# One weight split moved behind the layer norm, and two rounding copies moved from the vector to the scalar engine

## The chip, the cores and the metric

The kernel runs on one core of one Trainium2 chip. The metric is device time in microseconds (us) of one execution; lower is better. The engines of the core are TensorE (PE, with its weight loads listed as PEld), VectorE (DVE), ScalarE (ACT), GpSimd (POOL) and SyncE (SP, which issues most DMAs). Each engine runs its own instructions in the order in which the program gives them.

## The reference

One encoder layer for 1024 prompt frames, 64 sample frames and 16 meta tokens, all float32. A normed input goes through one projection into q, k, v, an attention gate, a GLU pair and a convolution gate. Group A is windowed attention. Group B is what this change touches; its reference is

```
def _conv_branch(u, left, conv_w, ln_g, ln_b, w_pw):
    h = _dwconv(jnp.concatenate([left, u], axis=1), conv_w)
    h = jax.nn.silu(_layernorm(h, ln_g, ln_b))
    return h @ w_pw
```

Both groups are then normed, multiplied by their gates, joined and multiplied by `w_out`; a last norm and the residual follow.

## The kernel before, in words

Float32 products are made of rounded parts. A weight or an activation is split into `hi` (the value rounded to the matmul's reduced float32 format, by a plain copy into a tile of that type) and `lo` (value minus `hi`, by a subtraction on DVE). A product is then three matmuls: hi with hi, hi with lo, lo with hi. So every operand of a matmul costs a copy and a subtraction before it may be used.

Four stages follow each other on PE. First the input projection: matmuls named `g`, in units of 24 (8 blocks of k, three parts) for each of 22 column blocks and 3 token ranges. From about 187 us on the attention (`s`, `pa`, `pb`, `av`) is woven between these units by a loop over `i`, 19 turns, in which `fill(n)` emits the next n projection matmuls. The same loop carries the layer norm of the convolution result `H` (128 partitions, 4 channel blocks, 1118 columns) in three token ranges: `ln_pre` (sums), `ln_mean`, `ln_var` (variance; DVE adds epsilon into `rln`, POOL raises it to the power -0.5), `ln_diag` (DVE writes the results on a diagonal, `sqc<-ident,rln`), and `ln_scale` (PE broadcasts them, `rstd<-sqc,ones_m`, and DVE multiplies, `H<-H,rstd`). The last range's `ln_var` comes at the end of the turn before last, its `ln_diag` and `ln_scale` in the last turn, i = 18.

The pointwise weights `w_pw` come in two blocks of 512 KB. The first, places 22 in `WORDER` (`whi`, `wlo`), is split as the projection ends. The second, place 23 (`w1kT` its hi, `w1vT` its lo), is split on DVE by `hi_w` and `lo_w` in turn 18, ahead of `ln_diag` and `ln_scale` of the last range.

After the loop `do` runs tasks by letters: `w` loads a block of `w_out`, `h` or `H` writes its hi part (on ACT or DVE), `l` its lo part on DVE and issues a later load, `S` is SiLU with the norm's gain and bias on `H` for one of four token ranges of 280 columns (ACT, 4 instructions), `z` is `split_z`, which splits that range into `zh` and `zl`, `g` is SiLU of a gate, `G` applies attention gates, `M` and `n` split the joined operand of the output product.

Then come the 16 pointwise products, n over four token ranges and m over four output blocks, 12 matmuls each (4 hi with `zh`, 4 lo with `zh`, 4 hi with `zl`). Behind each, DVE multiplies the result by the gate into `H` (`H<-pw,gb`, called H(n,m) here) and ACT squares it (`sqc<-pw` for m = 0, `csq<-pw` else, called square(n,m)). After each product the next item of a hand-written plan is emitted; a comma joins tasks of one item:

```
    plan = "G0,l1,h2 l2,h3 l3,S2 h4 z2 l4,h5 l5,S3 h6 z3,h7 l6,M0 l7 n0 r0 . M1 n1".split()
    for n in range(4):
        for m in range(4):
            pointwise(n, m, [pre[PW], pre[PW + 1]])
            do(plan[4 * n + m])
```

So `z2` follows product (1,0), and `z3` follows product (2,0). All of this is pinned to program order on each engine. Last comes the output product (`y` matmuls) for 9 token tiles, with its norm, residual and stores. All engine instructions pass through a helper, so DVE, ACT and POOL show line L86, matmuls L104, transposes L108.

Of the kernel before, what the change touches and what calls it, by code (L numbers as in the profile page):

```python
# [11 lines left out]
F32R = mybir.dt.float32r  # L12
AF = mybir.ActivationFunctionType
ALU = mybir.AluOpType

P = 128
# [6 lines left out]
KT = D // P  # L23
# [20 lines left out]
WORDER = [AT, BT, AT + 1, BT + 1, KM, AT + 2, BT + 2, VM, AT + 3, BT + 3] + [  # L44
    QT, QT + 1, QT + 2, QT + 3, GBT, GBT + 1, GBT + 2, GAT, GAT + 1, GBT + 3, GAT + 2, GAT + 3, PW, PW + 1]
# [3 lines left out]
def layer_kernel(ctx: ExitStack, tc: tile.TileContext, x, x_fm, w_in, w_pw, w_out, vec, g_post,  # L49
# [43 lines left out]
    act, dve, pool = Engine(nc.scalar, "act", 200, 0.82), Engine(nc.vector, "dve", 60, 1.18), Engine(nc.gpsimd)  # L93

    def freer():

        return "act" if given["act"] < (given["pe"] + LATE if taps else given["dve"]) else "dve"
# [16 lines left out]
    sm = ctx.enter_context(tc.tile_pool(name="sm", bufs=2))  # L114
# [21 lines left out]
    def slot(tag, name, shape=(P, 1152), dt=F32):  # L136
        return m4.tile(list(shape), dt, tag=tag, bufs=4 if tag == "B" else 2, name=name)
# [35 lines left out]
    def load_raw(p, parts=((0, KT),)):  # L173
        if p < len(WORDER) and (p not in raws or parts[0][0]):
            m = WORDER[p]
            src = w_in[m] if m < PW else w_pw[m - PW]
            if not parts[0][0]:
                raws[p] = wp.tile([P, KT, P], F32, tag="wraw", bufs=2, name=f"wraw{m}") if p != 2 else None
            for a, b in parts:
                if p == 2:  # L180
                    dst = halves[a] = sm.tile([P, 4, P], F32, tag="asq", bufs=2, name=f"wraw{m}_{a}")
                else:
                    dst = raws[p][:, a:b]
                nc.sync.dma_start(dst, src[:, a * P:b * P].rearrange("p (k c) -> p k c", c=P))
# [5 lines left out]
    def hi_w(p, on_dve=False, dst=None, a=0, b=KT):  # L190
        m = WORDER[p]
        load_raw(p)
        if not a:
            pre[m] = dst or (wp.tile([P, KT, P], F32R, tag="whi", name=f"whi{m}"),
                             wp.tile([P, KT, P], F32R, tag="wlo", name=f"wlo{m}"))
        raw, hi = halves[a] if p == 2 else raws[p][:, a:b], pre[m][0][:, a:b]
        if on_dve:
            dve.tensor_copy(hi, raw)
        else:
            act.activation(hi, raw, AF.Copy)  # L200

    def lo_w(p, a=0, b=KT, on_dve=False):
        hi, lo = (t[:, a:b] for t in pre[WORDER[p]])
        raw = halves[a] if p == 2 else raws[p][:, a:b]
        if p > 3 and not on_dve and freer() == "act":
            act.activation(lo, hi.bitcast(F32), AF.Copy, scale=-1.0)
            pool.dma_start(out=lo, in_=raw, accum_op=ALU.add)
            return
        dve.tensor_tensor(out=lo, in0=raw, in1=hi.bitcast(F32), op=ALU.subtract)
# [182 lines left out]
    def tick():  # L392
        steps[0] += 1
        run_due(lambda p: p[0] <= steps[0])
        while taps and given["dve"] < given["pe"] + AHEAD:
            f, j = taps.pop(0)
            f(j)

    def fill(k):
        for _ in range(min(k, len(queue))):  # L400
            queue.pop(0)()
            tick()
# [159 lines left out]
    def split_z(n):  # L562
        a, b = LNC[n]
        w = b - a
        hc = H[:, :, a:b]
        zh = slot("T", f"zh{n}", (P, 4, 280), F32R)
        zl = slot("P", f"zl{n}", (P, 4, 280), F32R)
        dve.tensor_copy(zh[:, :, :w], hc)
        dve.tensor_tensor(out=zl[:, :, :w], in0=hc, in1=zh[:, :, :w].bitcast(F32), op=ALU.subtract)
        zs[n] = zh, zl  # L570

# [119 lines left out]
    def att_v(c):  # L691

        if c % 2 == 0:
            nc.sync.dma_start(vE[MB:MB + HD], vtok[:HD, c // 2])
            avs[c] = [(NKEY, vE)]
            if c:
                avs[c].insert(0, (2 * HD, vcache if c == NCHUNK else vtok[:, c // 2 - 1]))
        else:
            if c > 1:
                nc.sync.dma_start(vO[:HD], vtok[HD:, c // 2 - 1])  # L700
            avs[c] = [(HD + MB, vO if c > 1 else vE), (NKEY, vtok[:, c // 2])]
# [17 lines left out]
    def att_values(c):  # L719
        sample = c == NCHUNK  # L720
        av = ps_tile("av", 1, f"av{c}")
        last = len(att[c]) - 1
        for n, (k, v, pt) in enumerate(att[c]):
            for g in range(2):
                mm(av[g * HD:(g + 1) * HD, :256], lhsT=v[:k, g * HD:(g + 1) * HD],
                   rhs=pt[:k, g * 256:(g + 1) * 256], start=n == 0, stop=n == last)
        av4 = av[:, :256].rearrange("p (t q) -> p t q", t=4)
        act.activation(qb[:, c], av4, AF.Copy)
        Tt = c // 2
        if Tt not in asq:  # L730
            asq[Tt] = sm.tile([P, 4, P], F32, tag="asq", bufs=2, name=f"asq{Tt}")
        o = (c % 2) * HD
        act.activation(asq[Tt][:, :, o:o + HD], qb[:, c], AF.Square)
        if c % 2 or sample:
            w = HD if sample else P
            s = asq[Tt]
            pool.tensor_tensor(out=s[:, 0:2, :w], in0=s[:, 0:2, :w], in1=s[:, 2:4, :w], op=ALU.add)
            pool.tensor_tensor(out=s[:, 0, :w], in0=s[:, 0, :w], in1=s[:, 1, :w], op=ALU.add)

    def att_stats(Tt):  # L740
        w = HD if Tt == 8 else P
        row_rstd(asq[Tt][:, 0, :w], w, ra[:, Tt:Tt + 1], f"ra{Tt}", mm_ps(f"ra{Tt}"))
# [139 lines left out]
    def gate_att(ready, most=12):  # L882
        for g in [g for g in gas if all(c in ready for c in range(g[2] // HD, g[3] // HD))][:most]:
            gas.remove(g)
            t, n, c0, c1, gt = g
            dst = qb[:, c0 // HD:c1 // HD, t, :]
            dve.tensor_tensor(out=dst, in0=dst, in1=chunks(gt[:, :c1 - c0]), op=ALU.mult)
# [64 lines left out]
    order = [NCHUNK] + list(range(NCHUNK))  # L952
# [5 lines left out]
    i = -1  # L958
    while (i := i + 1) < max(len(order) + 2, L0 + 7 if L0 < 99 else 0):
        left = len(order) + 1 - i  # L960
        if L0 == 99 and i >= 9 and (i == 12 or len(taps) < 2):
            L0 = i
        quota = (max(24, -(-(len(queue) - REST) // left)) if i else 48) if left > 0 else 26
        n = i - L0
        if i < len(order):
            exps, norm = att_scores(order[i])
        if n > 0:
            gate_att(order[:max(0, i - 2)], 2)
        if 3 <= i < len(order) + 3:
            c = order[i - 3]  # L970
            if c % 2 or c == NCHUNK:
                att_stats(c // 2)
        if 2 < i <= len(order) + 1:
            att_values(order[i - 2])
        if 1 < i < len(order):
            att_v(order[i])
        if i == len(order) + 1:
            hi_w(len(WORDER) - 1, on_dve=True, dst=[sm.tile([P, KT, P], F32R, tag=t, bufs=1, name=f"w1{t}")
                                          for t in ("kT", "vT")])
            lo_w(len(WORDER) - 1, on_dve=True)  # L980
        if i + 1 < len(order):
            att_prep(order[i + 1])
        fill((32 if i == 1 else 4) if left > 0 else 0)
        if 0 < i <= len(order):
            att_transpose(order[i - 1])
        if i < len(order):
            exps()
        fill(8 if left > 0 else 4)
        if n == 0:
            while taps:  # L990
                f, j = taps.pop(0)
                f(j)
            sqc = sm.tile([P, HW], F32, tag="sq", bufs=1, name="sqc")
        for step, at in ((ln_pre, (0,1,3)), (ln_diag, (2, 4, 6))):
            if n in at:
                step(at.index(n))
        if i < len(order):
            norm()
        fill(8 if left > 0 else 4)
        if i == 1:  # L1000
            att_values(order[0])
            att_v(order[1])
        for step, d in ((ln_mean, 0), (ln_var, 1), (ln_scale, 2)):
            if n - d in (0, 2, 4):
                fill(2)
                step((n - d) // 2)
        fill((quota - 20 if left > 0 else 8) - (2 if 0 <= n <= 6 else 0))

    def gb_silu(i):
        act.activation(gbs[i][:, :HW], gbs[i][:, :HW], AF.Silu)  # L1010
# [70 lines left out]
    def rc_rstd(T):  # L1081
        if T in rcs:
# [9 lines left out]
                 w=wo_load, G=lambda _: gate_att(order), H=lambda i: wo_hi(i, True))  # L1092
# [37 lines left out]
    for T in (0, 1, 8, 2, 3, 4, 5, 6, 7):  # L1130
# [40 lines left out]
        dst = y_p[t0:t0 + r] if T < 8 else y_s  # L1171
# [78 lines left out]
```

## Time and profile before

| what | value |
|---|---|
| median of 3 runs | 470.9 us (470.34 to 470.97) |
| the profiled execution: its own time | 470.69 us |
| its span, first to last instruction | 468.9 us |
| PE busy | 456.2 us (97%) |
| DVE busy | 380.1 us (81%) |
| ACT busy | 231.3 us (49%) |
| POOL busy | 75.0 us (16%) |
| mean granted TensorE clock | 0.997 |

The profiled execution takes 1.79 us more than its span and lies 0.21 us under the median. Busy shares are averages over stages with different limits, so the stage between 325 and 365 us has to be read by itself. In the listings below an instruction's start and duration are given, then its engine, the program's name of what is written and read, and in brackets the idle time of the engine before it with what ended it.

### The profile page before, as it was taken

The numbers are of one execution on the slowest core, as the hardware profiler recorded it, in microseconds if no ns is written. First come the engines' busy times: TensorE is split into PE (matmuls) and PEld (weight loads), VectorE is DVE, ScalarE is ACT, GpSimd is POOL, SyncE is SP. The second block draws the span as 40 slices with busy tenths as digits, with TensorE's granted clock in tenths as the row PEclk, the third lists the DMA queues.
The fourth block names the chain that finished last, engine by engine and source line by source line (L and its number), as shares of the span: only waits on it lengthen the run. The fifth ranks groups of instructions, "written<-read, shape, count | busy, mean of one in ns | idle before, by whom it ended". The sixth has DMA issues, their size and how long they took to land.

```text
span 468.9 us, 7427 instructions
## 1 busy us (share of the span) xinstructions
PE 456.2 (97%) x2809; PEld 416.7 (89%) x2809; DVE 380.1 (81%) x672; ACT 231.3 (49%) x534; POOL 75.0 (16%) x106
## 2 busy tenths in 40 slices
PE   7999999999999999999999999999999999999994
PEld 6999999999999999998988988797899787888884
DVE  3669999999999999999899987996999547554443
ACT  6585532135032223666766856774977335333322
POOL 0000100013000000010111113254024411111100
PEclk9999999999999999999999999999999999999998
DMA  8992144035023333330101010111252212222231
GB/s 271 402 344 117 36 105 126 0 86 153 13 68 93 89 91 91 89 94 5 48 7 49 6 52 4 48 55 42 97 175 90 91 67 91 67 92 90 97 124 48
DMA packets 16491, 43.54 MB, mean 93 GB/s; under 512 B 2600, under 2 KB 4888, under 8 KB 16456
## 3 DMA queue, kind: packets, MB, share of 16 engines
q1 hardware_dynamic: 14584, 37.31, 23.4%
q0 software_dynamic: 1872, 5.77, 6.6%
q8 instruction: 22, 0.36, 0.3%
q14 instruction: 13, 0.11, 0.1%
HBM read 32.00 MB, written 4.84 MB: 79 GB/s over the span
## 4 chain that ended last, share of the span: by engine, by line
PE 85%; DVE 8%; DMA 2%; ACT 2%; issue 1%; POOL 1%; SPq 0%; DVEq 0%; POOLq 0%; ACTq 0%
PE g L104 53%; PE y L104 20%; PE av L104 3%; PE s L104 3%; DVE wo L86 2%; DVE H L86 2%; PE pa L108 2%; PE pb L108 1%; DMA x<-in_x_fm_dram 1%; DMA woraw<-in_w_out_dram 1%; DVE wlo L86 1%; POOL sqc L86 1%; DVE qb L86 1%; DVE zl L86 1%; DVE sqc L86 0%
## 5 line engine op out<-in xcount | busy, mean ns | idle before, releaser
L104 PE MATMUL g<-xT,whi 128*128 128x384 f32 (+2 forms) x960 | 222.8, 332 | 1.1 <-ACT xT L86 0.9
L104 PEld LDWEIGHTS g<-xT,whi 128*128 128x128 f32 x960 | 168.3, 188 | 8.5 <-issue 5.4
L86 DVE SCALAR_TENSOR_TENSOR H<-u,vec_t,H 128x1118 f32<-128x1118 f32 x120 | 166.6, 1388 | 3.2
L104 PE MATMUL g<-xT,wlo 128*128 128x384 f32 (+2 forms) x480 | 139.1, 332 | 0.5 <-DVE wlo L86 0.5
L104 PEld LDWEIGHTS g<-xT,wlo 128*128 128x128 f32 x480 | 88.0, 188 | 2.7 <-issue 1.2
L104 PE MATMUL y<-wo,mh 128*128 128x512 f32 (+2 forms) x304 | 89.2, 381 | 0.0
L104 PEld LDWEIGHTS y<-wo,mh 128*128 128x128 f32 (+1 forms) x304 | 55.2, 185 | 11.5
L104 PE MATMUL y<-wo,ml 128*128 128x512 f32 (+1 forms) x136 | 51.3, 379 | 0.1
L86 DVE SCALAR_TENSOR_TENSOR y<-y,small,y 128x512 f32<-128x512 f32 (+1 forms) x19 | 13.7, 721 | 31.2 <-PE y L104 29.6
L86 ACT ACTIVATE T<-T,st 128x210 f32<-128x210 f32 (+2 forms) x84 | 36.6, 450 | 4.2 <-DVE st L86 4.1
L86 POOL DMA_DIRECT2D wlo<-wraw x13 | 11.5, 885 | 148.8 <-ACT wlo L86 112.9
L104 PEld LDWEIGHTS y<-wo,ml 128*128 128x128 f32 x136 | 25.6, 188 | 4.8 <-DVE ml L86 0.4
L86 ACT ACTIVATE yj<-y 128x512 f32<-128x512 f32 (+2 forms) x21 | 12.8, 609 | 31.8 <-DVE y L86 31.7
L86 ACT ACTIVATE whi<-wraw 128x1024 fp32r<-128x1024 f32 (+1 forms) x23 | 22.4, 978 | 6.3 <-PE g L104 6.1
L104 PE MATMUL g<-xT,wq 128*128 128x384 f32 (+1 forms) x144 | 25.4, 333 | 0.0
L104 PEld LDWEIGHTS g<-xT,wq 128*128 128x128 f32 x144 | 24.2, 188 | 0.5
L86 ACT ACTIVATE sg<-g 128x384 f32<-128x384 f32 (+1 forms) x10 | 4.7, 473 | 37.1 <-PE g L104 37.1
L86 ACT ACTIVATE qb<-g 128x384 f32<-128x384 f32 (+1 forms) x12 | 5.7, 474 | 32.1 <-PE g L104 32.1
L86 DVE CUSTOM_DVE_ANT_0 T<-s,bias 128x210 f32<-128x210 f32 (+2 forms) x68 | 20.6, 359 | 0.8 <-PE s L104 0.8
L86 ACT ACTIVATE y<-y,small 128x512 f32<-128x512 f32 (+1 forms) x19 | 12.6, 666 | 16.7 <-PE y L104 16.6
L86 POOL TENSOR_TENSOR asq<-asq 128x128 f32<-128x128 f32 (+2 forms) x18 | 12.7, 707 | 38.5 <-ACT asq L86 37.8
L86 ACT ACTIVATE qb<-av 128x256 f32<-128x256 f32 x17 | 6.4, 379 | 23.6 <-PE av L104 23.6
(199 smaller groups left out, 611.3 us busy)
## 6 DMA issues: line engine op xcount, KB each, us to landing
wraw<-in_w_in_dram SPq DMA_DIRECT2D x18, 512.0 KB, 3.4
wlo<-wraw POOLq DMA_DIRECT2D x9, 512.0 KB, 4.6
H<-in_x_dram SPq DMA_DIRECT2D x8, 512.0 KB, 8.2
xr<-in_x_dram SPq DMA_DIRECT2D x8, 512.0 KB, 4.0
out_dram<-o SPq DMA_DIRECT2D x7, 512.0 KB, 2.9
woraw<-in_w_out_dram SPq DMA_DIRECT2D x5, 512.0 KB, 3.3
wraw<-in_w_in_dram SPq DMA_DIRECT2D x8, 256.0 KB, 5.6
x<-in_x_fm_dram SPq DMA_DIRECT2D x4, 384.0 KB, 5.9
```

The source lines that it names most:

```text
L86: ins = op(*a, **k)
L104: return tc.keep_in_program_order(nc.tensor.matmul(out, lhsT=lhsT, rhs=rhs, **k))
L108: return tc.keep_in_program_order(nc.tensor.transpose(*a, **k))
```

## The change

The split of the second block of pointwise weights is emitted after the loop, so behind the last range's `ln_diag` and `ln_scale`. In `split_z` the rounded part of token ranges 2 and 3 is copied by ACT where DVE copied it; the subtraction stays on DVE.

```
@@ split_z
-        dve.tensor_copy(zh[:, :, :w], hc)
+        if n < 2:
+            dve.tensor_copy(zh[:, :, :w], hc)
+        else:
+            act.activation(zh[:, :, :w], hc, AF.Copy)
         dve.tensor_tensor(out=zl[:, :, :w], in0=hc, in1=zh[:, :, :w].bitcast(F32), op=ALU.subtract)
@@ loop over i
-        if i == len(order) + 1:
-            hi_w(len(WORDER) - 1, on_dve=True, dst=[sm.tile([P, KT, P], F32R, tag=t, bufs=1, name=f"w1{t}")
-                                          for t in ("kT", "vT")])
-            lo_w(len(WORDER) - 1, on_dve=True)
@@ behind the loop
+    hi_w(len(WORDER) - 1, on_dve=True, dst=[sm.tile([P, KT, P], F32R, tag=t, bufs=1, name=f"w1{t}")
+                                  for t in ("kT", "vT")])
+    lo_w(len(WORDER) - 1, on_dve=True)
```

## Rows read from the trace of the kernel before

**Rows 1.** The chain that ended last: start us, duration us, what.
```profile
326.71 1.23 DVE w1vT L86
...
365.00 8.24 PE y L104 x35
```
**Rows 2.** Windows: stretch, length, busy time of each engine, PEclk, DMA share, GB/s.
```profile
337.00:350.00 13.00, 12.83 (x99) 12.60 (x97) 12.90 (x22) 10.44 (x17) 2.70 (x3) 1.00 0.42 125
...
365.00:462.00 97.00, 97.00 (x457) 80.04 (x457) 49.38 (x94) 36.13 (x77) 15.03 (x21) 1.00 0.25 87
```
**Rows 3.** Timeline of PE, 329 to 359 us.
```profile
329.34 0.83 PE L104 MATMUL rstd<-sqc,ones_m 128*128 128x350 f32 x2 [0.74 <-DVE sqc L86]
...
338.27 0.69 PE L104 MATMUL pw<-zl,whi 128*128 128x280 f32 x4
...
350.01 0.79 PE L104 MATMUL pw<-zh,whi 128*128 128x280 f32 x4 [0.19 <-DVE zh L86]
...
351.84 0.78 PE L104 MATMUL pw<-zl,whi 128*128 128x280 f32 x4 [0.52 <-DVE zl L86]
...
358.82 0.77 PE L104 MATMUL pw<-zl,whi 128*128 128x278 f32 x4 [0.51 <-DVE zl L86]
```
**Rows 4.** Timeline of ACT, 334 to 357 us.
```profile
334.32 1.14 ACT L86 ACTIVATE gb<-gb 128x1118 f32<-128x1118 f32 x1
...
343.08 0.40 ACT L86 ACTIVATE sqc<-pw 128x280 f32<-128x280 f32 x1 [2.05 <-DVE H L86]
...
346.88 2.15 ACT L86 ACTIVATE H<-H,vec_t 128x280 f32<-128x280 f32 x4
...
349.29 1.14 ACT L86 ACTIVATE wo<-woraw,vec_t 128x1024 fp32r<-128x1024 f32 x1
...
352.18 0.40 ACT L86 ACTIVATE csq<-pw 128x280 f32<-128x280 f32 x1 [1.46 <-DVE H L86]
...
356.36 1.33 ACT L86 ACTIVATE wo<-woraw,vec_t 128x512 fp32r<-128x512 f32 x2
```
**Rows 5.** Timeline of DVE, 325 to 336 us.
```profile
325.43 0.68 DVE L86 CAST w1kT<-wraw 128x1024 fp32r<-128x1024 f32 x1
...
327.85 1.34 DVE L86 TENSOR_SCALAR sqc<-ident,rln 128x128 f32<-128x128 f32 x3
330.20 1.61 DVE L86 TENSOR_TENSOR H<-H,rstd 128x1400 f32<-128x1400 f32 x1 [1.01 <-PE rstd L104]
331.73 0.55 DVE L86 SCALAR_TENSOR_TENSOR ga<-ga,g 128x384 f32<-128x384 f32 x1
...
335.78 1.33 DVE L86 TENSOR_TENSOR zl<-H,zh 128x1120 fp32r<-128x1120 f32 x1
```
**Rows 6.** Timeline of POOL, the power for the last token range of the norm.
```profile
325.59 1.24 POOL L86 TENSOR_TENSOR rln<-rln,small 128x3 f32<-128x3 f32 x1 [1.71 <-DVE rln L86]
```
**Rows 7.** DMA of the blocks of `w_out`, asked by tile, from issue on.
```profile
DMA to landing us min/median/max: 2.7/3.2/4.8
```
**Rows 8.** Timeline of DVE, 349 to 365 us.
```profile
349.23 0.73 DVE L86 CAST zh<-H 128x1120 fp32r<-128x1120 f32 x1
349.99 1.79 DVE L86 TENSOR_TENSOR zl<-H,zh 128x1120 fp32r<-128x1120 f32 x1
351.71 0.44 DVE L86 TENSOR_TENSOR H<-pw,gb 128x280 f32<-128x280 f32 x1
...
356.98 1.79 DVE L86 TENSOR_TENSOR zl<-H,zh 128x1112 fp32r<-128x1112 f32 x1
358.69 0.43 DVE L86 TENSOR_TENSOR H<-pw,gb 128x280 f32<-128x280 f32 x1
...
363.67 1.27 DVE L86 TENSOR_TENSOR ml<-H,mh 128x512 fp32r<-128x512 f32 x1
```
**Rows 9.** SP's issue of one block of `w_out`, 342 to 347 us.
```profile
344.67 1.88 SPq L1030 DMA_DIRECT2D woraw<-in_w_out_dram  x2
```
**Rows 10.** A window of one us near the end of the span.
```profile
465.00:466.00 1.00, 0.00 (x0) 0.00 (x0) 0.77 (x2) 0.00 (x0) 0.00 (x0) 0.82 0.03 10
```

## The prediction

> **What bounds the kernel now.** I began with the chain that ended last. It runs through PE until about 326 us, then almost wholly through DVE until 365.00, and from there through PE to the end [rows 1]. The windows say the same: from 337 to 350 us DVE is busy for 12.90 of 13.00 us, and from 365 to 462 PE is busy for 97.00 of 97.00 [rows 2]. So the output product has no gap in which a delay could be made good: what moves its start at 365.00 moves the end by as much. The question is what the change does to that start.
>
> PE's own timeline shows five places before it where PE waits for DVE, four of them short: 0.74 us for the norm's diagonal, 0.19 for `zh` of range 2, 0.52 for `zl` of range 2, 0.51 for `zl` of range 3 [rows 3]; the fifth is the second `y` matmul at 365.00, which follows the end of DVE's `ml` [rows 1]. ACT is less busy than DVE here, but its timeline shows that it isn't free: its squares start only behind DVE's H(n,m), with ACT idle for 2.05 and 1.46 us in front of two of them [rows 4]. As ACT runs in program order, whatever makes DVE late also makes late all that stands behind a square on ACT.
>
> **Part 1, the weight split behind the norm.** DVE's work stays the same; only its order changes. The `hi` starts at 325.43 and takes 0.68, so 0.72 with the step to the next dependent instruction; the `lo` starts at 326.71 and the diagonal follows at 327.85, so 1.14 [rows 1, 5]: 1.86 us leave their place. The diagonal then waits for POOL's power, which ends at 325.59 + 1.24 = 326.83 [rows 6], and takes 1.34 [rows 5]: done at about 328.2, not 329.2. PE gets the broadcast `rstd` when it is free, 0.74 before 329.34, at 328.60 [rows 3]. The multiply on DVE follows `rstd` by 0.86 and takes 331.73 - 330.20 = 1.53 [rows 3, 5]: 329.46 to 330.99. Now come the 1.86 us: the gate `ga` starts at 332.85 where it started at 331.73 [rows 5]. DVE is 1.1 us later from here on, since two waits (for POOL and for PE) that the split used to cover are now open.
>
> Does PE feel that? PE is 0.74 earlier, but the third part of the first pointwise product needs `zl` of range 0, which moves from 335.78 to 336.9 and ends 1.33 later at 338.2; it started at 338.27 [rows 3, 5]. So PE's gain is given back at once, and PE is where it was. The load of `w_out` that waits for the split's source buffer now goes out at 332.85 on SP's queue, and lands at most 4.8 us later [rows 7], at 337.7. Its user on ACT stands behind three gates of 1.14 us, of which the first starts at 334.32 - 0.74, and four SiLU of 2.15 together [rows 4], so not before 338.9. The load is hidden; were it not, its lateness would fall on `h1` and so on square(0,0). Bounds of the shift: 0.95 if POOL's power ended as early as PE could use it, 1.86 if nothing of the waits is recovered. I take 1.1, as each wait has a row.
>
> **Part 2, the copy of range 2 on ACT.** DVE's copy starts at 349.23, takes 0.73, and PE starts on it at 350.01 [rows 3, 8]. On ACT the copy stands where `z2` stands in the plan: behind square(0,2), the SiLU of range 2, square(0,3), the `hi` of a block of `w_out` (`h4`) and square(1,0). The SiLU starts at 346.88 and `h4` at 349.29 [rows 4]; both hang on DVE through the squares and move by 1.1. The load for `h4` is issued at 344.67, when `l1` on DVE is done [rows 9], so now at 345.8, and lands between 2.7 and 4.8 us later [rows 7], at 350.6 at the worst; `h4` would start at 350.4, so at most 0.2 comes from there. `h4` takes 1.14, less an overlap of about 0.1: 351.4. Square(1,0) adds about 0.35: 351.75. The copy has 1120 columns; the nearest row is a gate of 1118 columns on ACT, 1.14 us [rows 4]. So `zh` is ready at 352.9, against 349.96 on DVE: 2.9 us later, of which 1.1 come from part 1. DVE, in order, does nothing from about 350.3 until then, and its subtraction follows. In the trace that takes 1.79 for this range and 1.33 for range 0 [rows 5, 8]; the longer one ran beside POOL, which will be done this time, so I take 1.33 with 1.25 to the next start. H(1,1) then starts at 354.15 and not 351.71 [rows 8]: 2.45 late. PE stands idle for some 3 us in front of product (2,0).
>
> The copy alone thus is no gain even where DVE is the bound: DVE is spared 0.76 us and then waits 2.6.
>
> **Part 2, the copy of range 3.** Square(1,1) follows H(1,1), so ACT is 2.45 late too, through the SiLU of range 3 and square(1,3) to `h6`: 356.36 becomes 358.8 [rows 4]. `h6` takes 1.33, less the overlap: 360.05. Square(2,0) brings 360.4, the copy 361.55, and the subtraction, again without POOL beside it, 362.8. In the trace it ended with the start of H(2,1) at 358.69 [rows 8]: 4.1 us late. PE idles again, about 2 us, in front of product (3,0).
>
> **The sum.** From there to the second `y` matmul the same chain remains: DVE's H, `l6`, `l7` and `ml`, whose last instruction starts at 363.67 [rows 8]. I take off 0.2 for less contention with POOL. So 1.1 (part 1) + 1.35 (range 2) + 1.65 (range 3) - 0.2 = 3.9 us on the start of `y`, and on the end: 470.69 + 3.9 = 474.6 us for an execution like the profiled one, which lay 0.21 under the median; between the two I say 474.7, 0.8% slower. The terms' bounds: part 1 from -0.15 to +0.75; each subtraction up to 0.46 more if POOL still runs beside it, together +0.9; `h4`'s load +0.2; the copies -0.1 each at the `hi` rate (1024 columns in 1.14), the tail -0.2. Low end 474.1, high end 476.5.
>
> **A rule of the Trainium skill.** The rows show that ACT's squares wait for DVE's read of the same result (1.46 us in front of square(1,1) [rows 4]). The Trainium skill, page "PSUM — Partial Sum Buffer", section "PSUM bank collisions raise a hardware error", says that two engines may not touch one bank at the same partitions at once, two reads included, and that the compiler back end therefore orders ACT against DVE. By that rule ACT stays behind DVE and the time is 474.7; without it the first rival below holds; the row agrees with the rule.
>
> **Rivals.**
>
> *ACT isn't held by DVE.* Were the squares tied only to PE, the chain would be free of DVE's 1.1 us. The next bound on ACT is the load for `h4`: issued at 345.8, landed 3.2 later at 349.0 [rows 7, 9]; `h4` until 350.05, `zh` at 351.5, H(1,1) 1.0 late, and with the same steps ACT reaches the second copy by 358.1: the start of `y` about 0.6 late, 471.3 us. Against it: both waits of rows 4.
>
> *ACT fills its gap* (the other side). ACT stands idle for 2.05 us in front of 343.08 [rows 4], and the columns that the SiLU of range 2 needs have been ready since 331.73 [rows 5]. If ACT's order on the chip let the SiLU and the copy slip forward there, both copies would be hidden. It decides at 349.9: `zh` of range 2 must be done by then, 3 us before my sum has it. DVE would be 1.1 late and 2 x 0.76 early, PE's waits of 0.19, 0.52 and 0.51 would mostly go, and the end would come about 1 us earlier: 469.7. Against it: in the trace the SiLU could have run in that gap and ran at 346.88.
>
> *The clock falls in PE's new stall.* In the trace the granted clock is 1.00 through the stretch to 462 [rows 2], and in the stretch 465 to 466, with PE doing nothing, it is 0.82 [rows 10]. My stall in front of product (2,0) is some 3 us, shorter than that. If the clock went to its lower level there, the 48 matmuls from the third part of product (2,0) to that of (3,0), which take 358.82 - 351.84 - 0.51 = 6.5 us [rows 3], would take up to 13; about 2.1 us of that lie in the second stall, so at most 4.4 come on top: 479; with half of it, 477. The Trainium skill, page "TensorE: Matmul & The Clock Gate", Part 1, holds that an idle array is put back to the half rate, so by that rule the stall might cost this; no row here shows a fall after a stall of that length.
>
> **How the numbers follow.** My forecast gets 0.79, the clock 0.10, the free ACT 0.06, the filled gap 0.05. A measurement of this kernel can tell about 0.2%, 0.9 us, from no change. So slower 0.89, same 0.06 (471.3 lies within), faster 0.05. The range has to take in the terms' bounds, and some room towards either neighbour for order effects that I could only time to some tenths at each of about ten steps: 473.0 to 476.9.
>
> **What would show it.** In the profile after: `rstd` on PE at about 328.6 with no wait; the multiply near 329.5 and `w1kT` behind it; `ga` near 332.9. `zh` of range 2 and 3 on ACT, starting near 351.8 and 360.4, behind a square and 1.0 to 1.2 us long. DVE idle ahead of both `zl`, 2.6 and 3.3 us. PE idle near 350 to 353 and 359.6 to 361.6. `y` running densely from about 369. The prediction is wrong if the ACT copies start before 350 and 357, if DVE isn't late from 333 on, or if the granted clock in 350 to 370 is under 1.

## The result and the profile after

The changed kernel takes 475.2 us (median of 4 runs, 475.0 to 476.34) where the kernel before, measured with it, takes 470.62 (470.3 to 470.97): a ratio of 1.0099, 95% interval 1.0086 to 1.0112. It is slower by 4.6 us. The prediction was 474.7, with 473.0 to 476.9 as its range.

The profiled execution took 476.34 us, with a span of 474.6, so it is the slowest of the four. To compare times inside two executions I take the last `var` matmul of the norm as zero, since all that the change touches comes behind it. It starts at 324.52 us in the kernel before and at 324.94 in the changed one: 0.42 us are to be taken off every time below. The first row is from PE's timeline before, the second from PE's timeline after.

```profile
324.52 0.67 PE L104 MATMUL var<-ones_m,sqc 128*128 128x2 f32 x6
```
```profile
324.94 0.67 PE L104 MATMUL var<-ones_m,sqc 128*128 128x2 f32 x6
...
328.86 0.75 PE L104 MATMUL rstd<-sqc,ones_m 128*128 128x350 f32 x2
...
343.06 0.79 PE L104 MATMUL pw<-zh,w1kT 128*128 128x280 f32 x4 [0.70 <-DVE ga L86]
...
353.10 0.78 PE L104 MATMUL pw<-zh,whi 128*128 128x280 f32 x4 [2.00 <-ACT zh L86]
...
361.67 0.79 PE L104 MATMUL pw<-zh,whi 128*128 128x278 f32 x4 [1.76 <-ACT zh L86]
...
363.02 1.29 PE L104 MATMUL pw<-zl,whi 128*128 128x278 f32 x4
...
370.35 0.39 PE L104 MATMUL y<-wo,ml 128*128 128x512 f32 x1
```

This answers to [rows 3]. The wait of 0.74 us for the diagonal is gone. The waits of 0.19 and 0.52 us in front of range 2 have become one of 2.00, now for ACT, and range 3 has got one of 1.76. The second `y` matmul starts at 370.35 - 0.42 = 369.93, where it was 365.00: 4.93 us late. DVE's `ml` isn't what it waits for here: that ends at 367.85 + 1.28 = 369.13 (rows below), and PE then runs without a gap, slowed by a lower clock that is taken up with the filled stalls. Behind `y` PE's work has not changed, as the windows show (stretch, length, busy time of PE, PEld, DVE, ACT, POOL, PEclk, DMA share, GB/s); this answers to the second of [rows 2]:

```profile
373.00:466.00 93.00, 93.00 (x438) 76.63 (x437) 46.19 (x88) 33.24 (x71) 12.15 (x18) 1.00 0.24 82
```

DVE's timeline after, which answers to [rows 5, 8]:

```profile
326.91 0.66 DVE L86 TENSOR_SCALAR sqc<-ident,rln 128x128 f32<-128x128 f32 x3 [0.97 <-POOL rln L86]
329.65 1.61 DVE L86 TENSOR_TENSOR H<-H,rstd 128x1400 f32<-128x1400 f32 x1 [2.08 <-PE rstd L104]
...
333.04 0.55 DVE L86 SCALAR_TENSOR_TENSOR ga<-ga,g 128x384 f32<-128x384 f32 x1
...
337.08 1.33 DVE L86 TENSOR_TENSOR zl<-H,zh 128x1120 fp32r<-128x1120 f32 x1
...
353.08 1.32 DVE L86 TENSOR_TENSOR zl<-H,zh 128x1120 fp32r<-128x1120 f32 x1 [2.47 <-ACT zh L86]
354.32 0.44 DVE L86 TENSOR_TENSOR H<-pw,gb 128x280 f32<-128x280 f32 x1
...
361.65 1.32 DVE L86 TENSOR_TENSOR zl<-H,zh 128x1112 fp32r<-128x1112 f32 x1 [3.24 <-ACT zh L86]
362.88 0.44 DVE L86 TENSOR_TENSOR H<-pw,gb 128x280 f32<-128x280 f32 x1
...
367.85 1.28 DVE L86 TENSOR_TENSOR ml<-H,mh 128x512 fp32r<-128x512 f32 x1
```

The two waits that the weight split used to cover stand open (0.97 us for POOL, where there was none, and 2.08 for `rstd`, where there was 1.01 [rows 5]), then come 2.47 and 3.24 us in which the bound engine waits for ACT's copies. ACT's timeline after, which answers to [rows 4], shows why the copies are late:

```profile
344.39 0.40 ACT L86 ACTIVATE sqc<-pw 128x280 f32<-128x280 f32 x1 [3.94 <-DVE H L86]
...
348.19 2.15 ACT L86 ACTIVATE H<-H,vec_t 128x280 f32<-128x280 f32 x4
...
350.59 1.14 ACT L86 ACTIVATE wo<-woraw,vec_t 128x1024 fp32r<-128x1024 f32 x1
...
351.91 1.14 ACT L86 ACTIVATE zh<-H 128x1120 fp32r<-128x1120 f32 x1
354.80 0.41 ACT L86 ACTIVATE csq<-pw 128x280 f32<-128x280 f32 x1 [1.75 <-DVE H L86]
...
358.97 1.33 ACT L86 ACTIVATE wo<-woraw,vec_t 128x512 fp32r<-128x512 f32 x2
...
360.48 1.13 ACT L86 ACTIVATE zh<-H 128x1112 fp32r<-128x1112 f32 x1
```

ACT is idle for 3.94 us behind DVE, and then everything in its queue stands in front of a copy for which DVE waits. The ring closes: DVE holds ACT, ACT holds DVE.

### The profile page after: what moved, and what is told of

The parts are those of the page before. It is cut to its first block, busy times and chain, and to the rows that moved or that the text cites. A ratio compares the mean times of both kernels' runs of the same rounds, so it can differ in the third digit from the quotient of the medians.

```text
span 474.6 us, 7427 instructions
## 1 busy us (share of the span) xinstructions
PE 458.3 (97%) x2809; PEld 418.0 (88%) x2809; DVE 377.3 (80%) x670; ACT 233.4 (49%) x536; POOL 74.0 (16%) x106
## 4 chain that ended last, share of the span: by engine, by line
PE 79%; DVE 7%; ACT 3%; issue 1%; POOL 1%; DVEq 0%; POOLq 0%; ACTq 0%
PE g L104 46%; PE y L104 20%; PE av L104 3%; PE s L104 3%; PE pw L104 2%; PE pa L108 1%; PE pb L108 1%; DVE H L86 1%; DVE wo L86 1%; ACT H L86 1%; POOL sqc L86 1%; DVE qb L86 1%; DVE zl L86 1%; ACT wo L86 1%; DVE wlo L86 0%
```

## The experiments

All runs were compared with runs of the kernel before on the same chip. "Late" is the time from the `var` matmul to the second `y` matmul in the profiled execution, less the 40.48 us that it takes before.

| run | `var` | second `y` | late, us | ratio to before, 95% interval |
|---|---|---|---|---|
| changed | 324.94 | 370.35 | 4.93 | 1.0099 (1.0086 to 1.0112) |
| split alone | 325.65 | 367.01 | 0.88 | 1.0018 (1.0010 to 1.0027) |
| copies alone | 324.55 | 367.93 | 2.90 | 1.0074 (1.0062 to 1.0086) |
| copy of range 2 alone | 324.81 | 366.81 | 1.52 | 1.0042 (1.0028 to 1.0055) |
| copies ahead of the hi part | 324.96 | 365.24 | -0.20 | 0.9995 (0.9985 to 1.0005) |
| stalls filled | 323.84 | 368.11 | 3.79 | 1.0087 (1.0075 to 1.0099) |
| copies of ranges 0 and 1 | 324.54 | 364.04 | -0.98 | 0.9973 (0.9962 to 0.9984) |
| squares first | 324.49 | 365.31 | 0.34 | 1.0038 (1.0025 to 1.0052) |
| all copies early | 324.12 | 363.41 | -1.19 | 0.9965 (0.9952 to 0.9977) |
| changed, again | 324.49 | 368.75 | 3.78 | 1.0089 (1.0074 to 1.0104) |
| stalls filled, again | 324.17 | 368.42 | 3.77 | 1.0084 (1.0071 to 1.0098) |
| late split, all copies early | 324.44 | 364.03 | -0.89 | 0.9982 (0.9972 to 0.9992) |

**The split alone.** The changed kernel with DVE's copy put back:

```
-        if n < 2:
-            dve.tensor_copy(zh[:, :, :w], hc)
-        else:
-            act.activation(zh[:, :, :w], hc, AF.Copy)
+        dve.tensor_copy(zh[:, :, :w], hc)
```

> The weight split alone stands behind the loop; all four rounded parts are copied on DVE, as before. By the sum of the prediction DVE is about 1 us late from the gate behind the split on (the changed kernel shows 0.9 us there) and nothing up to the output product recovers it: 0.9 to 1.1 us over the kernel before, 471.5 to 471.7. Rival: DVE's lateness lies in slack and PE keeps the 0.74 us that it no longer waits for the diagonal: no change or up to 0.7 us faster.

471.71 us, 0.18% over before, 0.88 us late. The first theory holds. The waits of ranges 2 and 3 are there as before, only later; two of them in PE's timeline of this run, and the `y` that follows `ml`:

```profile
353.85 0.79 PE L104 MATMUL pw<-zl,whi 128*128 128x280 f32 x4 [0.53 <-DVE zl L86]
360.84 0.78 PE L104 MATMUL pw<-zl,whi 128*128 128x278 f32 x4 [0.51 <-DVE zl L86]
367.01 0.50 PE L104 MATMUL y<-wo,ml 128*128 128x512 f32 x1
```

The 0.51 and 0.53 stand beside 0.51 and 0.52 in [rows 3]: PE doesn't lose the waits, it is shifted with DVE.

**The copies alone.** The kernel before with the new lines of `split_z`.

> The weight split is where it was; the rounded parts of ranges 2 and 3 are copied on ACT at their place in the plan. By the sum: 1.35 us for range 2 and 1.65 for range 3, less 0.2: about 2.8 us over before, 473.4; zh of range 2 starts on ACT near 350.7. If the granted clock falls in PE's stall as in the changed kernel, up to 1 us more. Rival: the copies cost little by themselves and only the late split makes ACT late: under 1 us over before.

474.12 us, 0.74% over: 0.7 us more than the 473.4 expected, though `y` is 2.90 us late in the profiled execution against the 2.8 of the sum (where a part of the difference lies is told under "What stays open"). ACT's copy of range 2 starts where the sum had it without the late split. So the copies cost by themselves, and 0.88 + 2.90 = 3.78 us is what DVE's chain loses in the changed kernel (3.76, below); what that kernel's profile has beyond it is the clock's. ACT's timeline of this run:

```profile
350.65 1.14 ACT L86 ACTIVATE zh<-H 128x1120 fp32r<-128x1120 f32 x1
```

**The copy of range 2 alone.** The condition reads `if n == 2` for ACT.

> The kernel before with only range 2's rounded part on ACT. If the cost of the two copies adds up as in the prediction's sum, this is 1.35 us of the 2.8: 472.0, with zh near 350.65 and DVE's copy of range 3 about 1.3 us late behind the SiLU. Rival: DVE's 0.42 us of waiting ahead of range 3 and the spared copy take it up: within 0.5 us of before.

472.8 us, 0.42% over (472.0 expected); 1.52 us late. DVE's `ml` is 1.30 late (365.26 - 324.81 against 363.67 - 324.52), as the sum had it; the rest is PE's own, which runs at a granted clock of 0.60 from 353 to 357 us (second fence, windows) and meets no second stall. The rival falls: DVE's wait of 0.42 us ahead of range 3's copy doesn't take it up, it is there again, 0.42, since the SiLU of range 3 comes later too:

```profile
357.81 0.74 DVE L86 CAST zh<-H 128x1112 fp32r<-128x1112 f32 x1 [0.42 <-ACT H L86]
...
365.26 1.27 DVE L86 TENSOR_TENSOR ml<-H,mh 128x512 fp32r<-128x512 f32 x1
```
```profile
353.00:357.00 4.00, 4.00 (x22) 3.97 (x21) 4.00 (x7) 3.10 (x6) 2.44 (x2) 0.60 0.24 70
```

**The copies ahead of the hi part.** The kernel before, with `split_z` parted into `Z` (ACT's copy) and `z` (the subtraction) for ranges 2 and 3:

```
-    plan = "G0,l1,h2 l2,h3 l3,S2 h4 z2 l4,h5 l5,S3 h6 z3,h7 l6,M0 l7 n0 r0 . M1 n1".split()
+    plan = "G0,l1,h2 l2,h3 l3,S2 Z2,h4 z2 l4,h5 l5,S3 Z3,h6 z3,h7 l6,M0 l7 n0 r0 . M1 n1".split()
```

> As the run with the copies alone, but ACT's copy of ranges 2 and 3 is emitted ahead of the hi part of the block of w_out that stood in front of it (right behind the square that follows the SiLU); the subtraction stays at its place. If what costs is the place in ACT's queue, zh is ready near 350.4 and 357.5, and the time is 470.6 to 471.3, at least 2 us under the run with the copies alone. Rival: a copy on ACT costs by its length and by the hop between engines wherever it stands: 473 and more.

470.56 us against 470.7: no difference that can be measured, and 3.1 us earlier at `y` than the copies alone. The same two instructions on the same engine cost 2.9 us or nothing by whether one other instruction of 1.1 to 1.3 us and a square stand in front of each. DVE still waits, 1.14 and 1.73 us. The two spared copies (0.73 and 0.74) alone don't pay for that: the subtractions start later, when POOL is done, and take 1.33 and 1.32 us where they took 1.79 beside it [rows 8], and the 0.42 us that DVE waited ahead of range 3 before is part of the 1.73:

```profile
350.90 1.33 DVE L86 TENSOR_TENSOR zl<-H,zh 128x1120 fp32r<-128x1120 f32 x1 [1.14 <-ACT zh L86]
...
357.95 1.32 DVE L86 TENSOR_TENSOR zl<-H,zh 128x1112 fp32r<-128x1112 f32 x1 [1.73 <-ACT zh L86]
```

**The copies of ranges 0 and 1.** The kernel before with `if n < 2` for ACT, the other two on DVE:

> The kernel before, with the rounded parts of ranges 0 and 1 on ACT instead of 2 and 3; the weight split where it was. Theory (what counts is whether ACT reaches the copy before DVE asks for it): here ACT makes each copy right behind its SiLU, done near 334.2 and 338.7, where DVE asks near 335.0 and 338.4; DVE is spared 1.5 us less some 0.4 us in which it waits for a later hi part of w_out: 1.1 us faster, 469.6. Rival: a copy moved from DVE to ACT costs more than it spares wherever it stands (1.14 us against 0.73): 471.5.

469.56 us, 0.27% faster; 0.98 us early. Here ACT makes the copies right behind their SiLU while DVE is busy with the split and the gates; DVE waits for the second for only 0.48 us:

```profile
335.03 1.32 DVE L86 TENSOR_TENSOR zl<-H,zh 128x1120 fp32r<-128x1120 f32 x1
...
338.94 1.32 DVE L86 TENSOR_TENSOR zl<-H,zh 128x1120 fp32r<-128x1120 f32 x1 [0.48 <-ACT zh L86]
```

**The squares first.** The changed kernel; in `pointwise` the square and its sum are emitted ahead of DVE's multiply of the same result.

> The changed kernel with one order turned round: behind each pointwise product ACT's square is emitted ahead of DVE's multiply of the same result, so DVE waits for ACT and not ACT for DVE. If ACT was late because it stands behind DVE, it now runs ahead up to its loads: zh of range 2 starts near 350.5 instead of 351.9, that of range 3 near 357 instead of 360.5, and the time is about 3.3 us under the changed kernel, 472. Rival: the squares wait for something else (the sum that they feed, the product itself): no change, 475.2.

472.72 us, 0.38% over before, against 0.99% for the changed kernel. The squares did wait for DVE's read. Turned round, ACT runs ahead until it meets its loads, as the row of `h4` says, and DVE now waits for a square (0.96 us, second fence, DVE's timeline of the same run):

```profile
348.94 1.15 ACT L86 ACTIVATE wo<-woraw,vec_t 128x1024 fp32r<-128x1024 f32 x1 [2.49 <-DMA woraw<-in_w_out_dram]
...
350.28 1.13 ACT L86 ACTIVATE zh<-H 128x1120 fp32r<-128x1120 f32 x1
```
```profile
350.41 0.45 DVE L86 TENSOR_TENSOR H<-pw,gb 128x280 f32<-128x280 f32 x1 [0.96 <-ACT sqc L86]
```

Both copies start where expected (350.28, and 356.85 for range 3). The prediction's first rival had `h4` bound by its load at 349.0 and the time at 471.3; made real, `h4` starts at 348.94 and this execution takes 471.34, but the 12 runs spread from 471.30 to 474.37, wider than any other kernel here. The seven with a mean granted clock of 0.994 or less average 473.2, the five at 0.996 or more 472.0; that is all the runs say of it. The Trainium skill, page "PSUM — Partial Sum Buffer", section "PSUM bank collisions raise a hardware error", has two engines' reads of one bank put in order; the trace agrees, since whichever read is emitted first, the other waits for it (3.94 us for ACT in the changed kernel, 0.96 us for DVE here).

**The stalls filled.** The changed kernel with extra matmuls, whose result nothing reads, at the start of ranges 2 and 3:

```
+        if n > 1:
+            fps = ps_tile("av", 1, f"fill{n}")
+            for _ in range(14 if n == 2 else 12):
+                mm(fps[:, :280], lhsT=pre[PW][0][:, 0, :], rhs=zs[n - 1][0][:, 0, :280], start=True, stop=True)
```

> The changed kernel, with 14 and 12 extra matmuls of 280 columns ahead of the products (2,0) and (3,0), into a bank that nothing reads, 1.8 and 1.5 us of PE inside its two stalls of 2.2 and 1.9 us. In the changed kernel's profile the granted clock is 0.50 from 363 to 366, under the products of range 3. If that fall comes from PE's idling and sets the start of the output product, the clock stays at 1.00 and the time falls by about 1 us, to 474.2. Rival: DVE's ml sets that start anyway: 475.2, whatever the clock.

In the changed kernel's profile the granted clock is at its lower level, 0.50, from 363 to 366 us, and four matmuls of range 3 take 1.29 us there in place of 0.77 [rows 3]. Windows of the changed kernel:

```profile
362.00:363.00 1.00, 1.00 (x8) 0.75 (x6) 1.00 (x2) 0.66 (x1) 0.00 (x0) 0.88 0.13 49
363.00:364.00 1.00, 1.00 (x5) 0.98 (x5) 1.00 (x3) 0.64 (x2) 0.16 (x1) 0.50 0.00 0
```

With the stalls filled the clock stays at 1.00 and `y` is 3.79 us late and not 4.93. But the time was 474.96, 0.87% over before, and not the 474.2 expected, and its interval overlaps that of the changed kernel. So both were run once more on one chip:

> The changed kernel once more, beside the next run on the same chip. Its time without the clock is 470.7 + 3.8 by the traces of the two parts alone (0.88 and 2.90 us on the start of the output product); with the clock's fall under range 2 or 3 it should lie at 475.0 to 475.5, mean granted clock 0.992 to 0.994.

> The changed kernel with both stalls filled, once more. If the clock's fall costs something in the median, this is 0.5 to 1.1 us under the run beside it, its mean granted clock is 0.995 to 0.997, and it lies 3.8 us over before, 474.5. Rival: the fall mostly lies under range 2 and is taken up by the second stall: no more than 0.3 us between the two.

474.99 and 474.83 us, 0.89% and 0.84% over: 0.16 us between the medians, as the rival has it, but with 4 and 5 runs and overlapping intervals a cost of 0.5 us isn't ruled out by the times alone. The windows of the two, the changed kernel first, show that the clock did fall again, this time under range 2 and not under range 3:

```profile
353.00:357.00 4.00, 3.94 (x21) 3.72 (x20) 4.00 (x5) 2.54 (x5) 1.87 (x2) 0.64 0.11 37
```
```profile
353.00:357.00 4.00, 3.95 (x30) 3.72 (x30) 4.00 (x6) 2.88 (x6) 2.21 (x2) 1.00 0.18 46
```

PE gets through 21 matmuls in place of 30, and the late products eat up the second stall: PE's last wait in this execution is 0.25 us, not 1.76, and `y` is 3.78 us late, as late as with the stalls filled (3.77).

**All copies early.** The plan with `Z2` and `Z3`, and ACT's copy for all four ranges; the split at its old place.

> The weight split where it was; all four rounded parts on ACT, ranges 0 and 1 right behind their SiLU and ranges 2 and 3 one square behind it, ahead of the hi part of w_out. DVE is spared four copies, 3.0 us. PE has only some 1.2 to 2 us of waits to give back in this stage, so PE becomes the bound: 469.0 to 469.6. Rival: ACT, now with 4.5 us more, becomes the bound through the hi parts and squares behind the copies: 470.6 or more.

469.25 us, 0.35% faster (0.23 to 0.48%), the fastest kernel of the study; `y` is 1.19 us early, and PE's last wait in the stage is 0.26 us, in front of range 3. PE is busy for 13.00 of 13.00 us from 337 to 350, DVE for 11.34:

```profile
337.00:350.00 13.00, 13.00 (x102) 13.00 (x102) 11.34 (x17) 12.56 (x20) 3.03 (x3) 1.00 0.48 160
```

**The late split on top of it.**

> All four copies early on ACT, as in the run that was 0.35% faster, but the weight split behind the loop as in the changed kernel. If DVE still sets the stage, the late split costs its 0.9 us again: 470.1, still at or under before. If PE or ACT has become the bound, the cost is less than 0.4 us: 469.2 to 469.6. A third way: PE's 0.74 us at the diagonal becomes a gain now that DVE is ahead, and the time falls under 469.

469.92 us, 0.18% faster than before. The third way is refuted: the late split brings nothing. By the ratios it costs 0.17% (0.8 us), by the two profiled executions 0.30 us; between "the old 0.9" and "less than 0.4" the runs don't decide. Both figures have the late split slower here too, but the two kernels' intervals overlap (0.9972 to 0.9992 and 0.9952 to 0.9977), so that is likely and not shown.

## Why the prediction was right

**The stage.** The start of `y` sets the end: the table shows it, each kernel's ratio going with its lateness, except for the squares-first kernel, whose runs spread widely. That DVE's chain sets this start is confirmed for the kernels with the split alone, the copies alone, the copies of ranges 0 and 1, the filled stalls and the changed kernel run again, where `y` follows `ml` as before. In the other profiles `ml` is done earlier and PE itself, running without a gap, sets it: by a fallen clock in the first profile of the changed kernel and with the copy of range 2 alone, by its own work where copies or squares come early.

**Part 1** was put at 1.1 us, with a `zl` of range 0 that gives PE's gain back at once. Measured: `ga` at 333.04 - 0.42 = 332.62, 0.89 late, and 0.88 at `y` in the run of the split alone. The power on POOL was shorter and the diagonal took 0.66 us and not 1.34, but that helped little, since PE wasn't free for `rstd` before 328.44, 0.16 sooner than the prediction had it; so the shift lies just under its lower bound of 0.95. `zl` of range 0 started at 336.66 (predicted 336.9). One thing was missed: product (0,3) waited 0.70 us, with DVE's late gate as its releaser. It cost nothing more here, because a longer stall follows in front of range 2.

**Part 2, range 2.** Predicted: the copy starts at 351.75 and H(1,1) is 2.45 late. Measured: 351.49, and 353.90, 2.19 late. DVE waited 2.47 us (2.6 predicted). The chain through the squares, SiLU, `h4` and square(1,0) was right, and the runs with the squares first and with the copies ahead of the hi part show both of its links.

**Part 2, range 3.** Predicted: copy at 360.4, H(2,1) 4.1 late. Measured: 360.06 and 3.77. DVE waited 3.24 us (3.3 predicted).

**The sum** was 3.9 us at `y`. DVE's `ml`, the last link, started 367.43 - 363.67 = 3.76 late; the two parts alone add up to 3.78; the changed kernel run again has 3.78. The sum was 0.1 too large, and that it came so close is in part luck: part 1 was put 0.2 too high and the two copies 0.1, and the 0.2 taken off for less contention with POOL wasn't there (from H(2,1) to the last `ml` it is 363.67 - 358.69 = 4.98 us before and 367.85 - 362.88 = 4.97 after). The forecast of 474.7 is 3.8 us over the median before, the measured time 4.6 over its own; about 0.4 us of the difference lies behind `y`, where the sum had no term.

**The clock** is the step that was wrong. I held that the stall was too short for a fall and gave it one chance in ten, and named a granted clock under 1 in 350 to 370 us as a sign that the prediction is wrong; it is 0.91 there in both profiles of the changed kernel. That the time still lay near the forecast is because the fall cost little: the prediction's price had the clock low under all 48 matmuls between the two stalls, and it was low from 363 to 366 us in one profile and between 354 and 358 in the other. The stall was shorter still, about 2 us, as PE had already lost 0.70 us in range 0; and the clock fell nevertheless. The price was wrong too, in the other direction: not 2.2 to 4.4 us but 1.15 us in one execution (4.93 - 3.78) and nothing at `y` in the other (3.78 against 3.77 with the stalls filled), where the fall came under range 2 and the stall in front of range 3 took it up, as the prediction had it do in part. With the copy of range 2 alone there is no such stall, and the fall cost 0.2 us (1.52 - 1.30). Between the medians of the filled and the unfilled kernel it is 0.16 us. The Trainium skill, page "TensorE: Matmul & The Clock Gate", Part 1, has an idle array put back to the half rate; the filled stalls agree with it, and what the kernel lost by it was small.

**What stays open.** Where copies of range 2 or 3 stand behind a hi part, the ratios are 0.2 to 0.6 us larger than the lateness of the profiled executions (0.89% of 470.9 is 4.2 us, against 3.78), and that of the squares-first kernel 1.4 us; only the first profile of the changed kernel is the other way, as its execution was the slowest of four. A good part of this lies behind `y`. From the second `y` matmul to the end of the span it is 104.2 to 104.3 us in the profiles of all these kernels, and 103.8 to 104.0 in the kernel before and all others. It is no engine's work: DVE's last two instructions start 2.68 to 2.69 us behind the last `y` matmul in every run, and the 0.4 us come after them, at the end of the program. No run here says why. What is left is some 0.2 us either way, and 1 us for the squares first, whose profiled execution (471.34) is among the fastest of its twelve.

## What to carry to other kernels

Before moving an instruction to the engine with less busy time, write down what stands in front of it in that engine's queue and what those wait for: two copies cost 2.9 us here or nothing by their place in one queue alone, and two others of the same length, which ACT reached in time, gained 1 us. An engine that follows the bound engine through shared results (here the squares behind DVE's reads) inherits its delays, and its idle time is no slack. Work that covers another wait on the bound engine isn't free to move: put behind the wait, it opens the wait and keeps its own length.

## What the runs showed of the hardware

The granted clock fell to 0.50 after PE stalls of about 2 us, while the products behind them were already running: in the copies-alone run PE waited 1.98 us up to 351.83, and the clock was 0.86 in 352 to 354 and 0.50 in 354 to 356 (windows of that run). In the same kernel it fell now under range 2, now under range 3, and what it cost followed from what stood behind it.

```profile
352.00:354.00 2.00, 1.94 (x12) 1.71 (x13) 2.00 (x3) 0.47 (x2) 0.00 (x0) 0.86 0.00 0
354.00:356.00 2.00, 2.00 (x11) 2.00 (x10) 2.00 (x3) 1.89 (x4) 1.69 (x2) 0.50 0.17 31
```

Not every stall of this length was followed by a fall: behind the 2.00 us in the first profile of the changed kernel the clock stayed at 1.00 from 353 to 361, and fell behind the 1.76. The waits of PE up to 0.81 us in this stage (squares first: 0.81 in front of range 2) brought none: the clock is 1.00 from 350 to 370 us there.

DVE's subtraction of 128x1120 took 1.79 us in the kernel before, where a sum on POOL had started first (349.54 to 350.61, the subtraction at 349.99 [rows 8]). It took 1.31 to 1.33 in all runs where none ran beside it, and 1.32 with the squares first, where POOL's started 0.34 us after it.
